# A trunk of two transformer layers on one core: adaLN weights ahead of x, a fourth query buffer, one held tile pair

## The chip, the core and the metric

The kernel runs on one core of one Trainium2 chip. Its time is the device time of one execution in microseconds (us). Three runs of the kernel before took 2890.32, 2893.75 and 2896.26 us; the median is 2893.75.

## The reference

Two layers of a diffusion trunk in float32: width 1024, 1024 latent tokens, 256 context tokens, feed-forward width 2816. Each layer takes six modulation vectors from a conditioning vector (adaLN), normalises, attends and runs a SwiGLU. Layer 0 attends in a sliding window, layer 1 in a neighbourhood of a 64-column grid; layer 1 leaves its context rows unchanged.

```python
h, hc = x, ctx
for i in range(2):
    sh1, sc1, gt1, sh2, sc2, gt2 = split(silu(c) @ w_ada[i] + b_ada[i], 6)
    # sh1c ... gt2c likewise from silu(c_ctx)
    a  = rms_norm(h, g_mix[i]) * (1 + sc1) + sh1
    ac = rms_norm(hc, g_mix[i]) * (1 + sc1c) + sh1c
    y, yc = (swa_mixer, na_mixer)[i](a, ac, ...)
    h = h + gt1 * y
    h = h + gt2 * swiglu(rms_norm(h, g_ffn[i]) * (1 + sc2) + sh2)
    # the context rows hc the same way, in layer 0 only
```

## The kernel before

Activations stand with the width on the 128 partitions and tokens in columns, in chunks of 512 tokens. Each float32 operand of a large product is split into a high and a low half (ACT writes the high one, the difference is taken by VectorE or POOL), and a product is three matmuls: high·high, high·low, low·high.

The stages follow each other in `run`: `front0` (modulation, projections), `attn0`, `back(0)` (output projection, feed-forward), `front1`, `attn1`, `back(1)`. All are written against pools of named tiles: `pool.tile(..., tag=, bufs=n)` gives one of n buffers, and whoever would fill a buffer waits until the last reader of its old content is done. A scheduler of the framework sets the order of instructions on each engine from the dependences, its own estimates and, where given, `high_priority`; `issue_after` keeps instructions behind another on their engine. The engines then run their own queues in order. SP (SyncE) issues nearly all transfers, one after the other.

Three places matter.

The start is `front0`. `load(0)` issues eight transfers of x (`xn`, 256 KB each) on SP; `stats` squares (ACT, L226 and L229) and adds (VectorE, L230); `modulate` sums over the partitions (PE, L238), takes the reciprocal root on POOL (L242), transposes (PE, L249) and then writes, for each of eight slices of 128 rows, a scaled tile `nt` (VectorE, L254), a high half (ACT, L259 or L263) and a low half `pr` (VectorE L260, or POOL L264). `ada_half(0, 0, half)` loads half of the first adaLN group, eight transfers of 512 KB (L176), and multiplies with the conditioning vector (L180), four products of 32 rows each for each of four steps, into one bank; `ada_close` copies it (ACT, L186), transposes (PE, L189) and adds the bias (VectorE, L196 to L202). `gsc` and `mod` from there are what `nt` and the halves are scaled and shifted with. `qkv_part` runs the first projections (PE, L354) on the halves. The rope tables are made on POOL (L425, L431).

In `attn1`, eight pairs of heads pass over eight query tiles of 128 tokens. `load_pair` loads values, the keys `kst1` of both heads (L667, three buffers) and the biases; `begin` loads the queries `qst1` of both heads for two query tiles at a time (L686 and L687, three buffers); `scores` multiplies (PE, L702 against the context's keys, L705 against the neighbourhood's) into a double bank `b2`, of which there are two, and takes the softmax (VectorE L710, ACT L712); `turn` transposes the probabilities (PE, L730); `finish` multiplies with the values (PE, L746) and the reciprocal sums (L752).

In `back`, gate and up are computed by a scheme that forms seven products of half-size blocks (`product`, PE L808) instead of eight. `first` makes the first two and keeps their results in two tiles `kp` (ACT, L967 and L970, eight buffers of the tag), `second` and `third` the other five. For the first NPRE = 6 of the 22 column blocks, `first` runs ahead of the others, since the second chunk of tokens is then still being normalised (L908). Of those six pairs, HELD stay in their tiles; the others are written to memory (L1026) and read back when their turn comes (L1040).

Of the kernel before, what the change touches and what calls it, by code (L numbers as in the profile page):

```python
# [12 lines left out]
F32R = mybir.dt.float32r  # L13
# [6 lines left out]
P = 128  # L20
# [30 lines left out]
def f32(ap):  # L51
    return ap.bitcast(F32)


class Trunk:
# [113 lines left out]
    def ada_half(self, layer, grp, half):  # L169
        nc = self.nc  # L170
        ps = self.bank()
        src = self.a["w_ada"][layer, :, grp * 2048:(grp + 1) * 2048].rearrange("(k p) (j n) -> k p j n", p=P, n=512)
        for k in range(4):
            w = [self.slot(F32) for _ in range(2)]
            for z in range(2):
                nc.sync.dma_start(out=w[z], in_=src[4 * z + k, :, half::2])  # L176
            for z in range(2):
                for i in range(2):
                    r = 64 * z + 32 * i
                    nc.tensor.matmul(ps[r:r + 32, :], self.cond[:, 4 * z + k, :], w[z][:, i], start=(k == 0), stop=(k == 3))  # L180
        self.ada_close(layer, grp, ps, [(half + 2 * i, (32 * i, 64 + 32 * i)) for i in range(2)])

    def ada_close(self, layer, grp, ps, parts):
# [184 lines left out]
    def front0(self):  # L368
        nc, tc, a = self.nc, self.tc, self.a
        with ExitStack() as cx:  # L370
# [3 lines left out]
            pool = self.pool(cx, "p1", 2)  # L374
# [3 lines left out]
            def load(c):  # L378
                c0, n = CH[c]
                for k in range(KT):  # L380
                    t = xpool.tile([P, 512], F32, name="x", tag="x")
                    nc.sync.dma_start(out=t[:, :n], in_=a["xn"][k * P:(k + 1) * P, c0:c0 + n])
                    xs[c, k] = t[:, :n]

            def stats(c):
                st = self.stat_start(tmp, CH[c][1], 2 - c // 2)
                for k in range(KT):
                    self.stat_add(st, xs[c, k])
                return st
# [3 lines left out]

            self.mod_pool = self.pool(cx, "p1m", MB)
            pts = [self.pair_tiles(c) for c in range(3)]
            load(0)
            sts = [stats(0)]
            mods = [modulate(0)]
            adv = lambda i, n: [next(mods[i]) for _ in range(n)]
            adv(0, 1)  # L400
            self.ada_half(0, 0, 0)
            adv(0, 4)
            units = [self.qkv_unit(0, 2, u) for u in range(2)]
            self.ada_half(0, 0, 1)
# [243 lines left out]
    def attn1(self):  # L648
        nc, tc, a = self.nc, self.tc, self.a
        with ExitStack() as cx:  # L650
            self.psum(cx, 4, 2)
            cx.enter_context(self.early)
            pool = self.early_pool
# [25 lines left out]
            def begin(pr, m):  # L679
                if m % 2 == 0:  # L680
                    qst = {}
                    for x in range(2):
                        h = 2 * pr + x
                        q = pool.tile([P, 2, 256], F32R, name="qst1", tag="qst1", bufs=3)
                        s = f32(self.qs[1][h * 64:(h + 1) * 64, :, m * P:(m + 2) * P])
                        nc.sync.dma_start(out=f32(q[0:64]), in_=s)  # L686
                        nc.sync.dma_start(out=f32(q[64:128]), in_=s)  # L687
                        qst[x] = q
                    cur["q"] = qst
                    cur["sm"] = self.small.tile([P, 2, 2], F32, name="sm1")  # L690
                    cur["two"] = {}
                lat = list(range(max(m - 1, 0), min(m + 2, 8)))
                return dict(cur, pr=pr, m=m, kts=lat + [8, 9] if m == 0 else [8, 9] + lat, nl=len(lat) * P, p=[], pt=[])
# [68 lines left out]
            for pr in range(8):  # L762
                load_pair(pr)
                for m in range(8):
                    if m % 2 == 1 and pr == 7:
                        self.wo_ahead.append(self.unit(a["w_o1"][len(self.wo_ahead)]))
                    u = begin(pr, m)
                    steps = list(range(0, len(prev["kts"]), 2)) if prev else []
                    for j in range(max(2, len(steps))):
                        if j < 2:  # L770
                            with tc.high_priority(offset=HP1):
                                scores(u, j)
                        if j < len(steps):
                            turn(prev, steps[j])
                    if old:
                        finish(old)
                    old, prev = prev, u
# [33 lines left out]
    def back(self, layer, o):  # L811
        nc, tc, a = self.nc, self.tc, self.a
# [165 lines left out]
        def weights(f):  # L978

            a11, a12, a21, a22 = load_gu(f, ((0, 0), (0, 1), (1, 0), (1, 1)))  # L980
            late = "vector" if f < NPRE else "gpsimd"
            if f >= NPRE:
                yield self.split(a11, xslot(), "vector"), self.split(a12, xslot(), "vector")
            s1 = self.add(wt(), a21, a22, ALU.add)
            s2 = sub(s1, a11)
            yield self.split(s2, xslot(), "vector")
            s3 = sub(a11, a21)
            rest = [self.split(x, xslot(), lo) for x, lo in ((s3, "vector"), (s1, late), (a22, late))]
            self.add(s2, a12, s2, ALU.subtract)
            yield rest + [self.split(s2, xslot(), late)]  # L990
# [15 lines left out]
            self.add(y1, y1, u3, ALU.mult)  # L1006
            nc.sync.dma_start(out=self.ss[layer][f, :, 512:1024], in_=y1)

        NPRE, HELD = 6, 2
        ew = []  # L1010
        for f in range(NPRE):
            a11, a12 = load_gu(f, ((0, 0), (0, 1)))
# [18 lines left out]
        for f in range(NF):  # L1031
            w = weights(f)
# [56 lines left out]
        for g in groups:  # L1089
            W = {f: self.unit(a["w_down"][layer, f * P:(f + 1) * P, :], alt(f), slot=self.slot if f > 1 else self.pslot) for f in g}  # L1090
            for c in range(2):
                acts = {}
                for f in g:
                    r = rawf()
                    nc.sync.dma_start(out=r, in_=self.ss[layer][f, :, c * 512:(c + 1) * 512])
                    w = self.split(r, self.pslot(), alt(f + 1))
# [185 lines left out]
```

## Time and profile before

| | |
|---|---|
| runs shown, median (us) | 2893.75 (2890.32 to 2896.26) |
| profiled execution, time (us) | 2896.47 |
| its span (us) | 2894.7 |
| its granted TensorE clock, mean | 0.992 |
| TensorE busy (us) | 2812.0 |
| VectorE, ACT, POOL busy (us) | 1645.7, 1119.7, 791.0 |
| HBM read, written (MB) | 317.73, 83.62 |

Times in the profile are microseconds from the start of the span. PE is TensorE, PEld its weight loads, DVE is VectorE, ACT ScalarE, POOL GpSimd, SP SyncE, and "SPq" work in SP's DMA queue. L354 is line 354 of the kernel before; three lines are added at L177, so that most lines of the kernel after have numbers higher by three. In a row of the timeline stand the start, the time until the last of the group ended, the engine, line and operation, the tile written and those read, shapes, and how many instructions the row holds; in brackets the idle time ahead of it and what ended that. In a row of waits stand the engine and line that waited, who ended it, the total in us, the times, and the longest.

### The profile page before, as it was taken

What the parts mean: (1) busy time and instruction counts of PE and PEld (TensorE: products, weight loads), DVE (VectorE), ACT (ScalarE), POOL (GpSimd) and SP (SyncE); (2) the same over time, 40 slices, a digit from 0 to 9 for tenths busy, and PEclk for the clock granted to TensorE, in tenths of its full rate; (3) what the DMA queues carried; (4) which work ended last, traced back from release to release, by engine and by line L of the source; (5) the groups of instructions that cost most, each with busy time, mean ns of one, the idle gap of its engine ahead of it and who ended that gap; (6) DMA issues with size and microseconds to landing.
All of it is one profiled execution on the core that took longest, in us unless ns stands there. A gap on an engine that the chain in (4) does not pass through costs nothing.

```text
span 2894.7 us, 42717 instructions
## 1 busy us (share of the span) xinstructions
PE 2812.0 (97%) x15586; PEld 2310.6 (80%) x15586; DVE 1645.7 (57%) x2965; ACT 1119.7 (39%) x2263; POOL 791.0 (27%) x802
## 2 busy tenths in 40 slices
PE   6999999999999999999999999999999999999999
PEld 3667777788888887778999888788788788887887
DVE  5657777658755555446543344166656856556442
ACT  4323666535223232234553222266654423233120
POOL 3443242210121222233873354111101021123220
PEclk8999999999999999999999999999999999999999
DMA  7583342434322248644563464366753422226221
GB/s 269 176 246 97 90 135 81 158 110 133 131 81 84 81 146 301 207 147 134 180 188 111 119 182 117 107 182 162 194 178 125 149 95 77 81 88 207 85 91 62
DMA packets 306178, 404.18 MB, mean 140 GB/s; under 512 B 30128, under 2 KB 165808, under 8 KB 305968
## 3 DMA queue, kind: packets, MB, share of 16 engines
q1 hardware_dynamic: 237072, 362.91, 39.7%
q10 hardware_dynamic: 68896, 38.55, 4.6%
q8 instruction: 123, 2.02, 0.3%
q14 instruction: 87, 0.71, 0.1%
HBM read 317.73 MB, written 83.62 MB: 139 GB/s over the span
## 4 chain that ended last, share of the span: by engine, by line
PE 87%; DMA 4%; DVE 4%; ACT 1%; issue 1%; POOL 1%; SPq 1%; DVEq 0%; ACTq 0%; POOLq 0%
PE b L808 17%; PE bm L1068 16%; PE bm L808 12%; PE bm L354 11%; PE bm L866 7%; PE bm L1129 4%; PE b L602 3%; PE b L354 3%; PE b L590 2%; PE b L1068 2%; DMA qst<-q_s 2%; PE b L730 2%; PE b L746 2%; PE b L557 1%; PE b L161 1%
## 5 line engine op out<-in xcount | busy, mean ns | idle before, releaser
L1068 PE MATMUL bm<-pr,wsp 128*128 128x512 f32 x1920 | 440.3, 390 | 0.0
L1068 PEld LDWEIGHTS bm<-pr,wsp 128*128 128x128 f32 x1920 | 359.2, 188 | 82.1 <-issue 5.9
L808 PE MATMUL b<-wsp,px 128*128 128x512 f32 x1584 | 377.9, 391 | 0.0
L808 PEld LDWEIGHTS b<-wsp,px 128*128 128x128 f32 x1584 | 297.5, 188 | 65.1
L848 DVE SCALAR_TENSOR_TENSOR px<-bm,mod,px 128x512 f32<-128x512 f32 (+1 forms) x232 | 170.7, 739 | 268.6 <-PE bm L1068 220.8
L808 PE MATMUL bm<-pr,px 128*128 128x512 f32 x1296 | 317.1, 392 | 5.2 <-ACT kp L970 5.2
L143 ACT CAST wsp<-raw 128x512 fp32r<-128x512 f32 x306 | 188.3, 620 | 342.5 <-PE bm L1068 116.3
L808 PEld LDWEIGHTS bm<-pr,px 128*128 128x128 f32 x1296 | 243.5, 188 | 59.3 <-ACT kp L970 6.1
L354 PE MATMUL bm<-wsp,pr 128*128 128x512 f32 x1152 | 272.4, 393 | 0.0
L144 POOL TENSOR_TENSOR px<-wt,px 128x512 fp32r<-128x512 f32 x64 | 91.1, 1424 | 628.5 <-ACT px L143 369.9
L354 PEld LDWEIGHTS bm<-wsp,pr 128*128 128x128 f32 x1152 | 213.4, 188 | 43.4
L144 POOL TENSOR_TENSOR wsp<-raw,wsp 128x512 fp32r<-128x512 f32 x132 | 174.7, 1331 | 250.4 <-ACT wsp L143 232.1
L143 ACT CAST px<-wt 128x512 fp32r<-128x512 f32 x176 | 108.3, 621 | 330.5 <-PE b L808 302.4
L144 DVE TENSOR_TENSOR wsp<-raw,wsp 128x512 fp32r<-128x512 f32 x174 | 141.2, 816 | 144.1 <-ACT wsp L143 143.0
L866 PE MATMUL bm<-pr,wsp 128*128 128x512 f32 x768 | 176.8, 390 | 0.0
L354 PE MATMUL b<-wsp,pr 128*128 128x512 f32 x576 | 148.8, 412 | 19.1 <-ACT pr L263 6.6
L866 PEld LDWEIGHTS bm<-pr,wsp 128*128 128x128 f32 x768 | 143.3, 188 | 29.3
L354 PEld LDWEIGHTS b<-wsp,pr 128*128 128x128 f32 x576 | 110.8, 198 | 56.2 <-issue 12.7
L710 DVE CUSTOM_DVE_ANT_0 pr<-b,wsp,big 128x640 f32<-128x640 f32 (+1 forms) x128 | 107.0, 847 | 83.9 <-PE b L705 71.5
L294 POOL TENSOR_TENSOR hrs<-hss,mhalf 128x8 f32<-128x8 f32 (+1 forms) x66 | 104.8, 1587 | 169.2 <-DVE hss L292 164.4
L1166 DVE TENSOR_TENSOR t<-b,kp 128x512 f32<-128x512 f32 x88 | 60.8, 691 | 135.5 <-PE b L808 135.2
L1129 PE MATMUL bm<-prc,wsp 128*128 128x256 f32 x1056 | 134.3, 285 | 0.0
(205 smaller groups left out, 4822.0 us busy)
## 6 DMA issues: line engine op xcount, KB each, us to landing
raw<-w_gu SPq DMA_DIRECT2D x156, 256.0 KB, 2.8
qst<-q_s SPq DMA_DIRECT2D x288, 128.0 KB, 3.1
rawf<-w_gu SPq DMA_DIRECT2D x132, 256.0 KB, 3.1
raw<-w_down SPq DMA_DIRECT2D x110, 256.0 KB, 3.3
wsp<-w_ada SPq DMA_DIRECT2D x48, 512.0 KB, 6.9
pr<-w_ada SPq DMA_DIRECT2D x48, 512.0 KB, 6.5
s_s<-t SPq DMA_DIRECT2D x88, 256.0 KB, 2.0
rawf<-s_s SPq DMA_DIRECT2D x88, 256.0 KB, 3.4
```

The costliest lines, as they stand in the source:

```text
L143: self.nc.scalar.copy(out=w[:, 0, :n], in_=x)
L144: getattr(self.nc, lo).tensor_tensor(out=w[:, 1, :n], in0=x, in1=f32(w[:, 0, :n]), op=ALU.subtract)
L294: nc.gpsimd.tensor_tensor(out=rs[:, :nh], in0=ss[:, :nh], in1=self.mhalf[:, :nh], op=ALU.pow)
L354: self.nc.tensor.matmul(ps, x, y, start=(k == 0 and i == 0), stop=(k == KT - 1 and i == 2))
L602: nc.tensor.matmul(op[64 * r:64 * r + 64, :256], u["v"][:, kts[i], :], u["pt"][i][:, 256 * r:256 * r + 256], start=(i == 0), stop=(i == n ...
L710: nc.vector.tensor_tensor_reduce(out=pt[:, :nl + 256], in0=V, in1=u["bias"][x][m // 7][:, b0:b0 + nl + 256], scale=-1.0, scalar=self.big, ...
L808: self.nc.tensor.matmul(ps, x, y, start=first and k == 0 and i == 0, stop=last and k == 3 and i == 2, skip_group_check=True)
L848: nc.vector.scalar_tensor_tensor(out=h[c, k], in0=ps, scalar=mod[:, ty, k, z:z + 1], in1=h[c, k], op0=ALU.mult, op1=ALU.add)
L866: nc.tensor.matmul(ps[:, :n], x, y, start=(k == 0 and i == 0), stop=(k == KT - 1 and i == 2))
L1068: nc.tensor.matmul(ps, x, y, start=(z == 0 and i == 0), stop=(z == len(parts) - 1 and i == 2))
L1129: nc.tensor.matmul(ps[:, q * CTX:(q + 1) * CTX], x, y, start=(k == 0 and i == 0), stop=(k == KT - 1 and i == 2))
L1166: self.nc.vector.tensor_tensor(out=out, in0=x, in1=y, op=op)
```

## The change

Four edits. In `ada_half`, the four products of a step are told to follow one another directly on PE, the second slot's pair first. In `front0`, `ada_half(0, 0, 0)` is written ahead of `load(0)`. In `attn1`, `qst1` has four buffers in place of three. In `back`, HELD is 1, so five pairs of the six are written and read back.

```diff
--- before.py
+++ after.py
@@ -174,10 +174,13 @@
             w = [self.slot(F32) for _ in range(2)]
             for z in range(2):
                 nc.sync.dma_start(out=w[z], in_=src[4 * z + k, :, half::2])
-            for z in range(2):
-                for i in range(2):
-                    r = 64 * z + 32 * i
-                    nc.tensor.matmul(ps[r:r + 32, :], self.cond[:, 4 * z + k, :], w[z][:, i], start=(k == 0), stop=(k == 3))
+            with ExitStack() as order:
+                for z in (1, 0):
+                    for i in range(2):
+                        r = 64 * z + 32 * i
+                        m = nc.tensor.matmul(ps[r:r + 32, :], self.cond[:, 4 * z + k, :], w[z][:, i], start=(k == 0), stop=(k == 3))
+                        if z and not i:
+                            order.enter_context(self.tc.issue_after(getattr(m, "ins", m)))
         self.ada_close(layer, grp, ps, [(half + 2 * i, (32 * i, 64 + 32 * i)) for i in range(2)])
 
     def ada_close(self, layer, grp, ps, parts):
@@ -393,12 +396,12 @@
 
             self.mod_pool = self.pool(cx, "p1m", MB)
             pts = [self.pair_tiles(c) for c in range(3)]
+            self.ada_half(0, 0, 0)
             load(0)
             sts = [stats(0)]
             mods = [modulate(0)]
             adv = lambda i, n: [next(mods[i]) for _ in range(n)]
             adv(0, 1)
-            self.ada_half(0, 0, 0)
             adv(0, 4)
             units = [self.qkv_unit(0, 2, u) for u in range(2)]
             self.ada_half(0, 0, 1)
@@ -681,7 +684,7 @@
                     qst = {}
                     for x in range(2):
                         h = 2 * pr + x
-                        q = pool.tile([P, 2, 256], F32R, name="qst1", tag="qst1", bufs=3)
+                        q = pool.tile([P, 2, 256], F32R, name="qst1", tag="qst1", bufs=4)
                         s = f32(self.qs[1][h * 64:(h + 1) * 64, :, m * P:(m + 2) * P])
                         nc.sync.dma_start(out=f32(q[0:64]), in_=s)
                         nc.sync.dma_start(out=f32(q[64:128]), in_=s)
@@ -1006,7 +1009,7 @@
             self.add(y1, y1, u3, ALU.mult)
             nc.sync.dma_start(out=self.ss[layer][f, :, 512:1024], in_=y1)
 
-        NPRE, HELD = 6, 2
+        NPRE, HELD = 6, 1
         ew = []
         for f in range(NPRE):
             a11, a12 = load_gu(f, ((0, 0), (0, 1)))
```

The order that the scheduler makes of it differs as follows at the places of which the prediction speaks. In SP's queue, at the start, `wsp` are the adaLN weights and `x` the tokens. Before:

```order
L85 DMA gm<-gains 128x32
L87 DMA bada<-b_ada 128x96
L382 DMA x<-xn 128x512 x8
L176 DMA wsp<-w_ada 128x2x512 x8
L131 DMA raw<-w_qkv 128x512 x3
L382 DMA x<-xn 128x512 x4
```

After:

```order
L85 DMA gm<-gains 128x32
L87 DMA bada<-b_ada 128x96
L176 DMA wsp<-w_ada 128x2x512 x8
L385 DMA x<-xn 128x512 x8
L131 DMA raw<-w_qkv 128x512 x3
L385 DMA x<-xn 128x512 x4
```

The two groups of eight have changed places. On POOL, at the start, `rot` and `rot_478` are the rope tables and `pr<-nt,pr` is a low half of the modulated tokens. Before:

```order
L242 TENSOR_TENSOR rs<-ss,mhalf 128x4
L144 TENSOR_TENSOR wsp<-raw,wsp 128x512
L425 TENSOR_TENSOR rot_478<-rot,gq 128x512
L264 TENSOR_TENSOR pr<-nt,pr 128x512
L431 TENSOR_TENSOR rot_478<-rot,gq 128x8x16 x4
L425 TENSOR_TENSOR rot<-rot,gq 128x512
L144 TENSOR_TENSOR wsp<-raw,wsp 128x512
L431 TENSOR_TENSOR rot<-rot,gq 128x8x16 x2
L264 TENSOR_TENSOR pr<-nt,pr 128x512
```

After:

```order
L144 TENSOR_TENSOR wsp<-raw,wsp 128x512
L245 TENSOR_TENSOR rs<-ss,mhalf 128x4
L428 TENSOR_TENSOR rot_478<-rot,gq 128x512
L434 TENSOR_TENSOR rot_478<-rot,gq 128x8x16 x4
L428 TENSOR_TENSOR rot<-rot,gq 128x512
L434 TENSOR_TENSOR rot<-rot,gq 128x8x16
L144 TENSOR_TENSOR wsp<-raw,wsp 128x512
L434 TENSOR_TENSOR rot<-rot,gq 128x8x16 x3
L267 TENSOR_TENSOR pr<-nt,pr 128x512 x2
```

A weight split stands ahead of the reciprocal root, and both tables stand ahead of the first low half. On PE, in `attn1`, at the first query tile of the second pair of heads, `kst_18083` and `kst_18092` (after: `kst_18089` and `kst_18098`) are the keys of the new pair's two heads, and the L730 rows transpose probabilities of the pair before. Before:

```order
L702 MATMUL b_18108<-kst_18083,qst_18101 128x256 x2
L705 MATMUL b_18108<-kst_18083,qst_18101 128x256 x2
L730 MATMUL b_18117<-ident,pr_18029 128x128
L730 MATMUL b_18117<-ident,pr_18045 128x128
L730 MATMUL b_18117<-ident,pr_18029 128x128
L730 MATMUL b_18117<-ident,pr_18045 128x128
L730 MATMUL b_18133<-ident,pr_18029 128x128
L730 MATMUL b_18133<-ident,pr_18045 128x128
L730 MATMUL b_18133<-ident,pr_18029 128x128
L730 MATMUL b_18133<-ident,pr_18045 128x128
L702 MATMUL b_18124<-kst_18092,qst_18104 128x256 x2
```

After:

```order
L705 MATMUL b_18114<-kst_18089,qst_18107 128x256 x2
L708 MATMUL b_18114<-kst_18089,qst_18107 128x256 x2
L705 MATMUL b_18130<-kst_18098,qst_18110 128x256 x2
L708 MATMUL b_18130<-kst_18098,qst_18110 128x256 x2
L733 MATMUL b_18123<-ident,pr_18035 128x128
L733 MATMUL b_18123<-ident,pr_18051 128x128
```

The second head's scores stand directly behind the first's, ahead of the eight transposes.

## Prediction

> **What bounds the kernel now.** I read the page's busy line and its chain first, then TensorE's waits over the whole span, then the timeline of the three places that the diff touches.
>
> ```profile
> PE 2812.0 (97%) x15586; PEld 2310.6 (80%) x15586; DVE 1645.7 (57%) x2965; ACT 1119.7 (39%) x2263; POOL 791.0 (27%) x802
> ...
> PE 87%; DMA 4%; DVE 4%; ACT 1%; issue 1%; POOL 1%; SPq 1%; DVEq 0%; ACTq 0%; POOLq 0%
> ...
> PE b L238 <- DVE acc L230: 15.2, 2, 13.0
> PE b L702 <- DMA qst<-q_s: 11.7, 12, 2.1
> PE b L354 <- ACT pr L263: 6.6, 2, 5.3
> ...
> PE bm L808 <- ACT kp L970: 5.2, 2, 2.6
> ...
> PE b L702 <- DVE ot L755: 1.2, 1, 1.2
> ```
>
> TensorE (PE) is busy for 97% of 2894.7 us, and the change leaves its instructions as they are; only idle time, or a low clock, can be won. All of it is 2894.7 − 2812.0 = 82.7 us, and the wait rows (line: us in total, times, longest) name what the diff reaches: 11.7 us in attention 2 for query tiles, 5.2 us in two pieces in the seven-product stage, and the start, where the wait on DVE `acc` and those around L354 lie.
>
> **Attention 2, the fourth query buffer.** The whole stage and its DMA queue:
>
> ```profile
> 1870.00:2128.00 258.00, 242.01 (x2415) 210.35 (x2415) 176.13 (x419) 172.17 (x419) 40.22 (x91) 1.00 0.61 164
> ...
> SPq L686 <- PE b L705: 85.8, 18, 38.8
> ...
> DMA to landing us min/median/max: 3.9/5.1/6.6
> ...
> DMA to landing us min/median/max: 3.9/4.4/4.8
> ```
>
> The columns of the first row are the window, its length, then busy time of PE, weight load, DVE, ACT and POOL, the granted clock (1.00) and the DMA share. PE idles 258.0 − 242.0 = 16.0 us, so no buffer here can bring more. The queue stands 85.8 us in front of query loads until scores (L705) free the third buffer: that is the cause of the 11.7 us. A fourth buffer lets both heads' next queries start one group of two query tiles earlier; such a group is 258/32 = 8.1 us, more than any landing in this stage took, so I take all 12 waits of 11.7 us as gone.
>
> What is late next? The keys `kst1`, which keep three buffers: at each of the seven boundaries between head pairs, the second head's keys are asked for only after the last use of a buffer of the pair before. The last two rows of the fence are the time from issue to landing of the key loads, in the whole stage and at the first boundary, which runs thus:
>
> ```profile
> 1898.23 1.11 SPq L667 DMA_DIRECT2D kst<-k_s  x2
> ...
> 1900.03 0.60 SPq L687 DMA_DIRECT2D qst<-q_s  x1
> ...
> 1902.74 0.48 PE L702 MATMUL b<-kst,qst 128*128 128x256 f32 x2
> 1903.30 1.04 PE L730 MATMUL b<-ident,pr 128*128 128x128 f32 x8
> ...
> 1905.99 0.48 PE L702 MATMUL b<-kst,qst 128*128 128x256 f32 x2 [1.65 <-DMA qst<-q_s]
> ```
>
> In the old order eight transposes (1.04 us) stand between the scores of the new pair's first head (1902.74) and those of its second; in the new order the second head's scores follow the first's at once, so PE asks for the second head's keys at 1903.30, not at 1904.34. Those keys are asked for at 1898.7 (second of the two issues) and land up to 4.8 us later, at 1903.5 to 1903.6: a wait of about 0.3 us remains. The same subtraction at the other six boundaries, each with its own landing, leaves 0.05, 0.3, 1.1, 0.4, 0.5 and 1.1 us; together 3.7 us. If all seven keys land as fast as the fastest (3.9), nothing is left; if all as late as the slowest (6.6), 1898.7 + 6.6 − 1903.3 = 2.0 us each, 14 us in all. I take 3.7, since it is the sum of landings that did occur, and the net is 11.7 − 3.7 = **8.0 us gained** (bounds: 11.7 + 1.2 for a wait put down to another engine, and −2.3).
>
> **The first adaLN weights ahead of x.** The rows of the start:
>
> ```profile
> 2.11 3.75 SPq L382 DMA_DIRECT2D x<-xn  x8
> 5.91 6.00 SPq L176 DMA_DIRECT2D wsp<-w_ada  x8
> ...
> 12.99 1.87 PE L238 MATMUL b<-ones,acc 128*128 128x2 f32 x8 [12.99 <-DVE acc L230]
> ...
> 15.21 1.02 POOL L242 TENSOR_TENSOR rs<-ss,mhalf 128x4 f32<-128x4 f32 x1 [13.91 <-DVE ss L240]
> ...
> 22.12 0.14 PEld L180 LDWEIGHTS b<-wsp,cond 128*32 128x32 f32 x4 [0.59 <-DMA wsp<-w_ada]
> ...
> 27.12 1.41 DVE L254 SCALAR_TENSOR_TENSOR nt<-x,gsc,b 128x512 f32<-128x512 f32 x2
> ...
> 29.85 2.07 PE L354 MATMUL b<-wsp,pr 128*128 128x512 f32 x4 [5.33 <-ACT pr L263]
> ...
> 31.04 1.71 POOL L264 TENSOR_TENSOR pr<-nt,pr 128x512 fp32r<-128x512 f32 x1
> ...
> 32.80 5.16 PE L354 MATMUL b<-wsp,pr 128*128 128x512 f32 x12 [0.88 <-POOL pr L264]
> ...
> 40.84 5.08 PE L354 MATMUL b<-wsp,pr 128*128 128x512 f32 x21 [1.04 <-POOL pr L264]
> ...
> 53.75 0.66 PE L189 MATMUL b<-ident,sb 128*128 128x128 f32 x4 [0.73 <-ACT sb L186]
> ```
>
> The swap moves 2 MB of x (8 × 256 KB) behind 4 MB of weights (8 × 512 KB) on SP's queue; `nt` (27.12) needs both, and both end near 22.1, where PE took up the last weights, either way. What follows the last landing differs. Before, it was the adaLN product, its copy, transposes and modulation sums: 22.1 to 27.1. After, it is the last Square and sum, the statistics product (L238, 1.9), the 1.0 us reciprocal root on POOL, now behind a 1.4 us weight split, and the transposes, which I put at the root's 1.0; I walk this to `nt` at about 28.5, and with the same hi half behind it to a first projection product near 32.0 in place of 29.85. On POOL, the rope tables move ahead of the first lo half:
>
> ```profile
> 29.42 1.66 POOL L425 TENSOR_TENSOR rot<-rot,gq 128x512 f32<-128x512 f32 x1 [2.56 <-DVE gq L420]
> ...
> 32.71 2.16 POOL L431 TENSOR_TENSOR rot<-rot,gq 128x128 f32<-128x128 f32 x4
> 34.84 1.27 POOL L425 TENSOR_TENSOR rot<-rot,gq 128x512 f32<-128x512 f32 x1
> 36.07 1.75 POOL L144 TENSOR_TENSOR wsp<-raw,wsp 128x512 fp32r<-128x512 f32 x1
> 37.79 1.77 POOL L431 TENSOR_TENSOR rot<-rot,gq 128x128 f32<-128x128 f32 x2
> ```
>
> Before, the first lo half stood behind one of these (ready at 32.75); after, behind 1.66 + 2.16 + 1.27 + 1.75 and four L431 at 0.89 (3.5), 10.4 us, and its own 1.3. From about 28.0, when VectorE has scaled `gq`, that is 39.7, seven microseconds later, and near the 40.84 at which PE took up its second lo half before. Products held back by it: 44 at 5.08/21 = 0.24 us, 10.6 us, with three groups of four adaLN products at about 1.0: 39.7 + 10.6 + 3.0 = 53.3. PE comes from a pause, and the clock comes in:
>
> ```profile
> 32.00:36.00 4.00, 3.20 (x8) 2.52 (x9) 2.62 (x4) 1.92 (x4) 4.00 (x6) 0.50 0.96 301
> 36.00:38.00 2.00, 2.00 (x10) 1.34 (x12) 2.00 (x2) 1.09 (x2) 2.00 (x3) 0.64 1.06 407
> 38.00:40.00 2.00, 1.80 (x12) 0.28 (x10) 1.61 (x3) 1.01 (x2) 2.00 (x3) 1.00 1.04 392
> ```
>
> The last column but two is the granted clock: 0.50 until PE has run without a break from 32.80 to about 37.4, 4.6 us that do 2.3 us of work: 53.3 + 2.3 = 55.6 against 53.75, **1.8 us lost** at the transposes (L189) on which the second half of the modulation hangs. [...]
>
> Keeping the column tiles together pays some of it back: four kept together take 1.0 us, and before, the second half ran its 16 in six pieces, now in four; that is already in the three groups above. The copy that the transposes waited for (0.73) has other products behind which to stand. I give back 0.8 us: **1.0 us lost** at the start. Bounds: 2 us gained, if the first lo half comes at 36.7, with POOL's tables begun 3 us sooner; 4 us lost, if the clock stays at half for over twice the 4.6 us.
>
> **One held pair in the seven-product stage.** Four more transfers of 256 KB go out per layer and come back (two each way), on SP's queue. The wait that holding two pairs could be the cause of:
>
> ```profile
> 682.14 0.72 ACT L908 ACTIVATE px<-px,mod 128x512 f32<-128x512 f32 x1 [1.08 <-DVE px L900]
> ...
> 688.96 0.57 ACT L970 ACTIVATE kp<-bm 128x512 f32<-128x512 f32 x1
> 689.59 0.79 PE L808 MATMUL bm<-pr,px 128*128 128x512 f32 x1 [2.61 <-ACT kp L970]
> ...
> 689.50:692.70 3.20, 3.11 (x7) 2.44 (x8) 3.20 (x7) 3.20 (x8) 0.00 (x0) 0.50 0.43 164
> ...
> kp<-u_s SPq DMA_DIRECT2D x16, 256.0 KB, 3.5
> ```
>
> PE's bank waits for an evacuation (L970) that stands in ACT's in-order queue behind modulation work; ACT runs without a gap from 682.14 to 688.96. No kept tile is awaited there, and in both programs PE, ACT and DVE have the same order up to it. So the 2.61 us, and the half clock behind it (3.2 us at 0.50, 1.6 us of work), stay in both layers. Behind this wait PE has no gap in the stage, so the reload of the second pair costs **nothing** while it lands before its use, and the pair before it has seven products to cover it. If that cover is gone, the price is one landing, the last row's 3.5 us, in one layer or in both. Bounds: 0.5 gained, 7 lost; I take 0, because PE waits for no reload of the pairs that are spilled already.
>
> **The sum.** −8.0 + 1.0 + 0 = −7.0. The profiled execution took 2896.47 (span 2894.7 and 1.8 around it), 2.7 above the median of the runs, 2893.75; I take the difference from the median: **2886.8 us**.
>
> **Rivals.**
> - *Everything gained.* The keys are hidden, because early queries leave the queue to them: 11.7 + 1.2 and a start that costs 1: 2893.75 − 11.9 = 2881.9. For: in the old order each key load stood behind query loads at its boundary. Against: landings of up to 6.6 us under a DMA share of 0.61.
> - *The keys take it back.* At each boundary 1.5 us for keys, 10.5 in all; with the start at 1 the result is 2893.5, no change. For: the new order asks earlier. Against: only one of the seven subtractions comes to over 1.1.
> - *Slower.* The new order puts both heads' scores side by side, where transposes stood between them, and there are two double banks: the next scores wait until a softmax pass (L710) has read one. If each of the 64 units of a pair and a query tile pays 0.22 us, the loss of 14.1 is over the 8.0 gained by 6.1, and with the start at 1 it is 2900.8. It decides from (8.0 − 1.0 + 5.8)/64 = 0.20 us a unit. Against: VectorE is busy 176.1 of 258 us, and the longest of PE's waits on it there is the 1.2 us above.
> - *The held pair was the wait.* If its two kept tiles hold ACT up, 5.2 us and twice 1.6 of clock go too: 8.4 more, 2878.4. Against: ACT had no gap.
> - *The start gains.* The adaLN work off the last landing is worth more than the lo half costs: 3 us gained in place of 1 lost, 2882.8. Against: the lo row.
>
> **Chances.** Forecast, net gain between 4 and 11: 0.52. Everything gained 0.12, keys take it back 0.15, slower 0.08, held pair 0.06, start gains 0.07. About 0.2%, 5.8 us, is what a measurement of this kernel can tell from no change; so faster begins at 2888.0. My forecast lies only 1.2 us beyond it: of its 0.52, 0.34 is faster and 0.18 same. Faster: 0.34 + 0.12 + 0.06 + 0.07 and 0.02 of the keys' case, 0.61; same: 0.18 + 0.12, 0.30, slower: 0.08 and 0.01 of the keys' case, 0.09. The range leaves out slower, held pair and a quarter of the keys' case: 2879.5 to 2893.0.
>
> **What would show it.** In the profile after: the wait of L705 (was L702) on `qst` gone or below 1 us, a new one on `kst` of 3 to 4 us at boundaries; PE busy in the attention window unchanged at 242 with 8 us less span; the wait on ACT `kp` still 5.2 in two pieces; the transposes of the first column's second half at 55 to 56. Wrong if `kst` waits exceed 8 us, if DVE appears as a releaser of scores, or if the start moves by over 4 us.

## The result, and the profile after

The changed kernel took 2874.29 us, the median of four runs (2872.16 to 2878.33), against 2895.01 for the kernel before beside it: a ratio of 0.9934 (95% interval 0.9922 to 0.9946), 20.7 us faster. Forecast were 7 us and a range of 2879.5 to 2893.0. A second set of five runs (e9 below) gave 0.9930 (0.9917 to 0.9942). The page's busy line and its chain, after:

```profile
PE 2805.8 (98%) x15586; PEld 2307.1 (80%) x15586; DVE 1641.8 (57%) x2965; ACT 1117.6 (39%) x2263; POOL 789.0 (27%) x802
...
PE 87%; DVE 3%; DMA 2%; ACT 1%; issue 1%; POOL 1%; SPq 0%; DVEq 0%; ACTq 0%; POOLq 0%
```

TensorE does the same work in a span of 2871.4 instead of 2894.7 us: 65.6 us of idle time where there were 82.7, and 6 us less at work. On the chain, transfers fall from 4% to 2% and VectorE from 4% to 3%. Four of PE's waits over the span (line: us in total, times, longest); the first is the start, where PE now waits for weights before it waits for x:

```profile
PE b L181 <- DMA wsp<-w_ada: 12.8, 5, 8.3
...
PE bm L811 <- ACT kp L973: 5.2, 2, 2.6
...
PE b L749 <- ACT ptt L516: 4.0, 1, 4.0
...
PE b L705 <- DMA kst<-k_s: 0.7, 1, 0.7
```

No wait for query tiles is left at L705 (11.7 us before, at L702). The wait in the seven-product stage is the same 5.2 us, the row on keys reads 0.7 us and not 3.7, and the wait of 4.0 us at L749 was 0.5 us before (L746). The window of attention 2, with the columns of the row shown for before:

```profile
1857.00:2107.00 250.00, 242.58 (x2425) 213.09 (x2424) 174.87 (x420) 171.11 (x421) 40.41 (x91) 0.99 0.65 169
```

To see where the 20 us came from, the span is cut at instructions that both programs have: the transposes of the second adaLN half (L189), the first scores of attention 1 (L557), its last product (L602), the first scores (L702) and the last product (L746) of attention 2. Lengths in us, worked out from PE's first and last instruction of each stage, for before, after and the kernels with some of the four edits:

| kernel | to L189 | rest of the first stage | attention 1 | attention 2 |
|---|---|---|---|---|
| before | 53.8 | 216.0 | 278.9 | 254.2 |
| e4, one held | 53.9 | 217.6 | 273.3 | 254.5 |
| e3 and e13, four query buffers | 53.9, 54.2 | 215.3, 214.8 | 276.8, 276.1 | 242.4, 241.0 |
| e2, tiles together | 52.9 | 216.0 | 273.9 | 257.6 |
| e1, weights first | 55.8 | 211.2 | 274.2 | 254.8 |
| e15, both at the start | 53.2 | 209.1 | 274.1 | 255.8 |
| e5, after with three query buffers | 54.7 | 209.4 | 275.4 | 253.0 |
| after and e9 | 53.2, 53.2 | 209.8, 209.5 | 273.7, 275.6 | 244.4, 244.3 |

The stages that are left out differ by at most 4 us between any two of these kernels, and follow no edit. Attention 2 is 253 to 258 us with three query buffers and 241 to 244 with four. The rest of the first stage is 215 to 218 with x loaded first and 209 to 211 with the weights first. Attention 1 differs by 5.6 us between before and e4, whose orders are the same on every engine up to there: that part of the difference between the two first profiles (5.2 us) belongs to no edit.

### The profile page after: what moved, and what is told of

It is laid out like the page before. It is cut to its first block, busy times and chain, and to the rows that moved or that the text cites. A ratio compares the mean times of both kernels' runs of the same rounds, so it can differ in the third digit from the quotient of the medians.

```text
span 2871.4 us, 42752 instructions
## 1 busy us (share of the span) xinstructions
PE 2805.8 (98%) x15586; PEld 2307.1 (80%) x15586; DVE 1641.8 (57%) x2965; ACT 1117.6 (39%) x2263; POOL 789.0 (27%) x802
## 4 chain that ended last, share of the span: by engine, by line
PE 87%; DVE 3%; DMA 2%; ACT 1%; issue 1%; POOL 1%; SPq 0%; DVEq 0%; ACTq 0%; POOLq 0%
PE b L811 16%; PE bm L1071 16%; PE bm L811 12%; PE bm L357 11%; PE bm L869 7%; PE bm L1132 4%; PE b L605 3%; PE b L749 3%; PE b L733 2%; PE b L593 2%; PE b L1071 2%; PE b L357 2%; PE b L708 1%; PE b L560 1%; PE b L705 1%; PE b L562 1%
## 5 line engine op out<-in xcount | busy, mean ns | idle before, releaser
L357 PE MATMUL b<-wsp,pr 128*128 128x512 f32 x576 | 147.3, 410 | 12.5 <-ACT kv L440 5.3
```

The source lines that it names most:

```text
L357: self.nc.tensor.matmul(ps, x, y, start=(k == 0 and i == 0), stop=(k == KT - 1 and i == 2))
```

## The experiments

**The four edits one at a time.** e1: the call of `ada_half(0, 0, 0)` ahead of `load(0)`.

```diff
+            self.ada_half(0, 0, 0)
             load(0)
...
-            self.ada_half(0, 0, 0)
```

> Only ada_half(0, 0, 0) is written ahead of load(0). Theory A (what the changed kernel gained ahead of attention 2, 12 to 13 us of span, comes from the new order at the start): 8 to 12 us faster than before, the waits at 111.6 (weights, 2.27 us) and at 151.0 (1.89 us) gone, first scores of attention 1 at 263 to 265 instead of 269.8. Rival B (these stalls come and go from run to run, whatever the kernel): no difference in the median, and the half-clock intervals behind the stalls fall in other places. Rival C (the order at the start gains only through the column tiles): within 2 us of before.

Measured: 2889.53 us against 2893.58, ratio 0.9981 (0.9972 to 0.9990). The start is 2 us longer, the stage behind it 5 us shorter. Theory A's waits are gone, its size is about half; rival B falls for this stage: every kernel with x first and the stage otherwise unchanged shows these waits, and in those with the weights first the wait for the weights and the later of the two on `hx` are gone, and the other is 0.6 us or less (0.9 in e16 and 1.1 in e12). PE's waits between 54 and 270 us, of before:

```profile
PE b L354 <- DVE hx L298: 4.4, 6, 1.9
PE b L161 <- DMA wsp<-w_ada: 2.5, 2, 2.3
```

The same view of e1, in which L161 is not named any more:

```profile
PE b L354 <- DVE hx L298: 1.8, 5, 0.6
```

e2: the column tiles alone.

```diff
-            for z in range(2):
-                for i in range(2):
+            with ExitStack() as order:
+                for z in (1, 0):
+                    for i in range(2):
...
+                        if z and not i:
+                            order.enter_context(self.tc.issue_after(getattr(m, "ins", m)))
```

> Only the column tiles of the adaLN half product are kept together; x is still loaded ahead of the weights. Theory A: 0 to 3 us faster, since only the second half's sixteen products change their place (six pieces become fewer), and the start up to 37 us with its 10.2 us at half clock stays. Rival C: 8 to 12 us faster, with the waits at 111.6 and 151.0 gone. Rival B: no difference in the median.

Measured: 2892.64 us, ratio 0.9993 (0.9985 to 1.0002), 1 us at L189 and nothing behind it (the wait at 111 us is 2.57, that at 150 us 1.63), which is what theory A expected and rival C did not. What the 1 us is, two rows of the timeline of before show: two products (x4, since the trace counts two matmuls for each, 64 at L180 for 32 products) take as long as four (x8).

```profile
45.85 1.05 PE L180 MATMUL b<-wsp,cond 128*32 128x512 f32 x4
...
51.95 1.06 PE L180 MATMUL b<-wsp,cond 128*32 128x512 f32 x8
```

e3: four query buffers alone; e13 is the same kernel again.

```diff
-  q = pool.tile([P, 2, 256], F32R, name="qst1", tag="qst1", bufs=3)
+  q = pool.tile([P, 2, 256], F32R, name="qst1", tag="qst1", bufs=4)
```

> Only qst1 has four buffers. Theory A: attention 2 is 8 to 10 us shorter, its query waits (12, 11.7 us) gone, and everything ahead of it is as before: the half-clock intervals near 27, 112, 372 and 392 us are there again. Rival B: one or more of these intervals is missing, though the order ahead of attention 2 is unchanged. A wait of about 4 us on an ACT copy near the last pair of heads, as in the changed kernel, if it comes from the early queries; if it is missing, it came from somewhere else.

> Only four query buffers, again. Theory A (the whole gain lies in attention 2, 10 to 12 us): 2880 to 2883 us. Rival N (it is larger than the stage shows, as the first six runs had it): 2876 to 2879 us. Attention 2 at 242 to 245 us in both.

Measured: 2878.27 against 2893.58 us, ratio 0.9945 (0.9930 to 0.9960); again 2880.05 against 2895.93, 0.9949 (0.9936 to 0.9963). This edit is three quarters of the whole. PE's waits of e3 in attention 2:

```profile
PE b L746 <- ACT ptt L513: 2.3, 1, 2.3
PE b L702 <- DMA kst<-k_s: 1.5, 3, 0.9
PE b L702 <- DVE mn L710: 1.1, 2, 0.9
```

The query waits are gone, the key waits are small. The two ratios mean 15 to 16 us, and the stage itself is 11.8 and 13.2 us shorter than before's; the interval of the second, 10.7 to 18.5 us, holds both.

e4: one held pair.

```diff
-        NPRE, HELD = 6, 2
+        NPRE, HELD = 6, 1
```

> Only HELD is 1. As predicted: within 1 us of before, the waits on ACT kp at L808 2.6 us in each layer as before. The rival (the held pair caused these waits): 5 to 9 us faster. Rival B: half-clock intervals ahead of the seven-product stage differ from before, though its order is unchanged.

Measured: 2893.71 us, ratio 1.0001 (0.9991 to 1.0010), and the wait on ACT `kp` unchanged at 5.2 us in two pieces. Nothing, as forecast.

**Do they add up?** e5 is the changed kernel with `bufs=3` again, e15 the kernel before with both edits at the start.

> The changed kernel with three query buffers again. Theory A (the edits add up: four query buffers 12 to 15 us, the two edits at the start 4 to 6, the held pair 0): 4 to 6 us faster than before, attention 2 at 254 to 257 us as before. Rival D (the start's edits gain only together, and the query buffers less than they did alone): 8 to 12 us faster than before.

> The two edits at the start alone (weights first, column tiles together), three query buffers, two held pairs. If edits add up: 5 to 7 us faster than before, the stage between 54 and 270 us at 209 to 211 us instead of 215 to 218, attention 2 as before.

Measured: e5 2887.11 against 2893.32 us, 0.9978 (0.9969 to 0.9988); e15 2886.70 against 2895.93, 0.9966 (0.9956 to 0.9976): 6 and 10 us, with intervals that overlap; e15 is above its expected 5 to 7. With the query buffers' 15 that makes 21 to 25, against 20.7 measured, so a plain sum is good enough. Rival D is not borne out, as e1 gained without the tiles and e5's median lies below 8 us; that a few microseconds come only from the two edits together is not excluded, since e5's interval reaches 9 us and e15's 13.

**Early loads, or another order of scores?** With four buffers the scheduler also orders the scores otherwise, so e10 and e14 keep the buffers and make the second head's load wait, e10 for a POOL copy of the previous group's reciprocal sums (`rx`), e14 for its plain sums.

```diff
+   if x and "last" in cur:    # e10; cur["last"] is the previous rx
+       nc.gpsimd.tensor_copy(out=q[0:1, 0, 0:1], in_=cur["last"][0:1, 0:1])
+   if x and "sm" in cur:      # e14, in place of these two lines
+       nc.gpsimd.tensor_copy(out=q[0:1, 0, 0:1], in_=cur["sm"][0:1, 1, 0:1])
    nc.sync.dma_start(out=f32(q[0:64]), in_=s)
```

> The changed kernel with its four query buffers, but the second head's query load waits for a POOL copy of the previous group's reciprocal sums, which is about as late as three buffers let it start. Theory I (the gain is the earlier start of the query loads): the query waits return, attention 2 is 252 to 258 us, 8 to 13 us slower than the changed kernel. Rival J (the gain comes from the scheduler's other order of scores, which four buffers bring): within 3 us of the changed kernel.

> The changed kernel with four query buffers, the second head's query load held back until the previous group's sums of the first head are there, earlier than in e10 by one softmax and a reciprocal. Theory I (the start of the query loads is what counts): the loss is much smaller than e10's 79 us, 5 to 25 us, and the stage has waits on qst again. Rival J (the scheduler's order of scores): within 3 us of the changed kernel, or as slow as e10.

Measured: e10 2951.59 us, 1.0204 of before (1.0190 to 1.0218); e14 2912.75 us, 1.0065 (1.0052 to 1.0077): 79 and 39 us slower than the changed kernel, both far more than expected; attention 2 takes 318.3 and 279.1 us. PE's waits of e14 in attention 2, now at L707:

```profile
PE b L707 <- issue: 15.3, 9, 4.3
PE b L707 <- DMA qst<-q_s: 10.3, 7, 2.3
PE b L735 <- ACT pr L717: 4.1, 14, 0.3
```

The query waits are back (10.3 us here, 10.6 in e10), near the 11.7 us of before, and the longer hold costs more; rival J's "within 3 us" falls. But the hold also made the scheduler order the scores anew, and most of the loss is in waits that neither kernel has. So it is shown that query loads held back bring the query waits back; how much of the gain the new order has by itself is not shown, and no kernel here has the one without the other.

**The wait of 4 us on a copy.** It stands in the timeline of after, in the last pair of heads. With three query buffers it is 0.8 us or less; with four buffers alone it is 2.3 us (e3) and 2.0 (e13), so it comes with the fourth buffer:

```profile
2052.43 2.04 SPq L131 DMA_DIRECT2D raw<-w_o  x3
...
2059.40 0.62 ACT L143 CAST wsp<-raw 128x512 fp32r<-128x512 f32 x1 [4.76 <-DMA raw<-w_o]
...
2060.23 0.36 ACT L516 COPY ptt<-b 128x256 f32<-128x256 f32 x1
...
2060.64 2.00 PE L749 MATMUL b<-ptt,v 128*64 128x128 f32 x20 [4.00 <-ACT ptt L516]
```

PE waits for a copy; the copy stands behind a cast of the next stage's weight in ACT's queue and began 0.2 us after that cast ended, and ahead of the cast ACT has idled for 4.76 us until the cast's transfer landed, 6.9 us after its issue, behind keys, biases and queries. e6 takes these weights ahead from query tile 3 of the last pair on, e7 and e11 write the first of them one pair earlier.

```diff
-   if m % 2 == 1 and pr == 7:
+   if m % 2 == 1 and pr == 7 and m > 1:                                    # e6
+   if (m % 2 == 1 and pr == 7 and m > 1) or (pr == 6 and m == 7):          # e7, e11
```

> The changed kernel, but in the last pair of heads the first output weights are taken ahead from query tile 3 on, not from tile 1 (three units ahead instead of four). Theory E (the 4 us wait on ACT's copy near 2060 us is a weight cast standing in ACT's in-order queue until its transfer has landed behind biases, keys and the now earlier queries): that wait and the half clock behind it go, attention 2 is 3 to 6 us shorter than 244.4, and 2 to 5 us of it stay in the whole. Rival F (ACT is simply short of time there): the wait stays, or moves, and the time is within 2 us of the changed kernel.

> The changed kernel, but the first unit of output weights is written in the pair before the last, so four units stay ahead. Theory E: the order of transfers puts this weight behind the biases all the same, so the cast waits as before if it stands at the same place in ACT's queue: 0 to 3 us faster. Rival F: no change.

> The changed kernel once more, beside the next three on the same chip. 2872 to 2878 us, attention 2 at 244 to 245 us with the wait on ACT's copy of about 4 us near 2060.

> The changed kernel with the first unit of output weights written one pair of heads earlier, beside the changed kernel. Theory E (its cast no longer stands in ACT's queue ahead of a copy that PE needs): attention 2 at 240 to 242 us, no half clock there, 3 to 6 us faster than the changed kernel. Rival K (its one shorter profile was chance): the same as the changed kernel within 2 us.

Measured: e6 2876.51 us, and its wait stays (3.04 us): the first cast still stood ahead of the copy that PE needs, and its transfer landed at 2062.0, so the edit moved nothing that counts. e7 2873.44 and e11 2873.76 us; the wait is gone in both, and attention 2 is 240.6 and 240.9 us. PE's waits of e11 there:

```profile
PE b L705 <- DVE mn L713: 1.9, 3, 0.9
PE b L705 <- DMA kst<-k_s: 1.3, 3, 0.9
```

That the cast in ACT's queue is the cause is shown by these two against e6: the wait goes only where the cast no longer stands there. Yet the whole gains nothing that these runs tell: e9, the changed kernel beside e11, took 2872.54 us (2869.91 to 2875.53), e11 2870.34 to 2876.14. Their ratios to before, 0.9930 and 0.9935, each have an interval of about 4 us to either side, so a gain as small as the stage's 3.6 us is neither shown nor excluded.

**The wait on ACT `kp`.** e12 takes e11 and moves eight additions of `norm_lat` from ACT to POOL, e16 four of them.

```diff
-   nc.scalar.activation(out=h[1, k], in_=h[1, k], func=AF.Identity, bias=sh[:, k, 0:1])
+   nc.gpsimd.tensor_scalar(out=h[1, k], in0=h[1, k], scalar1=sh[:, k, 0:1], scalar2=None, op0=ALU.add)
```

> As the one before, and the eight additions of a shift to the second chunk's tokens in back (ACT, L908's neighbour) are done by POOL, which is idle there. Theory L (the wait of 2.6 us on ACT kp in each layer is ACT's in-order queue of modulation work, whatever is held): both waits shrink to under 1 us, with their half clock, 4 to 9 us faster than the kernel before it. Rival M (POOL's slower additions come late for combine): a new wait on DVE or POOL in the products behind, and no gain or a loss.

> As e12, but only four of the eight shift additions go to POOL. Theory L: the waits on ACT kp shrink to about 1 us and no new wait of 1.9 us on DVE takes their place; 2 to 6 us faster than the changed kernel. Rival M: the wait is shared out between ACT and DVE as in e12, no gain.

Measured: e12 2871.89 us, 0.9929 (0.9916 to 0.9941) of before; e16 2872.05 us, 0.9918 (0.9904 to 0.9931). PE's waits of e12 in that stage of layer 0:

```profile
PE bm L811 <- DVE pr L144: 1.9, 1, 1.9
PE bm L811 <- ACT kp L973: 0.7, 1, 0.7
PE bm L811 <- DVE px L144: 0.5, 1, 0.5
```

ACT's wait falls from 2.6 to 0.7 us when its queue is shorter, which is theory L's mechanism, and VectorE's splits are late next: 3.1 us in all, rival M's result. e16 shares 1.4 and 1.6. Both ratios lie within the interval of the changed kernel's second set (0.9917 to 0.9942); none is shown to beat it.

**Is the stall at 111 us the gain at the start?** e8 leaves the start as before and begins the background adaLN products two query tiles later.

```diff
-                if layer == 0 and (ci or t > 2):
+                if layer == 0 and (ci or t > 4):
```

> The kernel before, with the start untouched, but the background adaLN products of the first stage begin two query tiles later. Theory G (of the 4.9 to 6.3 us that the weights-first order gained between 54 and 270 us, most is the weight wait near 111 us of 2.3 to 2.6 us, the two waits on DVE hx near 142 and 151, and their half clock): these waits shrink or go with the start as before, and the stage is 2 to 6 us shorter. Rival H (the gain comes from the start's new order itself): the stage keeps its 215 to 218 us.

Measured: 2890.33 us, 0.9990 (0.9981 to 0.9998). The waits on `hx` fell from 4.4 to 1.0 us, the weight wait stayed (2.5), and the stage kept 215.5 us, as rival H has it; but PE worked 2.2 us longer in it, where the products came in more and smaller pieces (two took as long as four in the rows under e2, 1.05 and 1.06 us), and the longest of the waits that G is about did not go. So e8 does not tell G from H. That the stage gains through these waits is read from the traces (from before to after its idle time falls from 18.4 to 12.5 us, its length from 216.0 to 209.8, and the two wait rows shown for before lose 5.2 us together); no experiment took them away alone, so this cause is argued and not shown.

## Why the prediction was wrong, point by point

**The query buffers: right mechanism, mis-sized.** The term was −8.0, from −11.7 for query waits and +3.7 for keys. The query waits went in full, but 11.7 us was too small a price for them. The idle time in a row begins at the end that the profile gives the instruction ahead, and that end can lie behind the start of the next one, here by 0.24 us. Two rows of after, with nothing awaited:

```profile
2073.50 1.03 PE L733 MATMUL b<-ident,pr 128*128 128x128 f32 x8
2074.29 0.48 PE L705 MATMUL b<-kst,qst 128*128 128x256 f32 x2
```

The scores start 0.79 us behind the first of eight transposes, though the row of the eight lasts 1.03. By that step the scores of 1905.99 in before were 1.90 us late, where the row says 1.65. Counted from start to start in the same way, the twelve query waits of before cost some 14.5 us (an estimate from the steps of ten profiles). Two waits on VectorE (`ot` 1.2 and `ri` 0.9 us) went too.

The key term held better than its row tells. At all seven boundaries of after, the second head's keys landed 4.6 to 5.3 us after their issue, and its scores started 0.1 to 0.25 us behind the landing: the keys did become the next thing that was late. Start to start this makes some 2.9 us in after, and 2.5 to 3.5 in e3, e13 and e9, close to the 3.7 of the walk; the rows (0.7 to 2.2 us) leave out the part ahead of the end that the profile gives and waits under 0.15 us, and put two of the waits of after down to other causes.

The copy behind the cast (2.0 to 4.0 us, with half clock behind it in after, 0.50 from 2061.2 to 2064.5, in e9, 0.68 from 2063.5 to 2067.0, and in e3, 0.99 over the stage where before has 1.00) is a wait that the prediction did not have, and it goes the other way. Together the stage is 10 to 13 us shorter than before's, where 8.0 was forecast, and the runs with four buffers alone give 15 to 16. The last 3 us lie within what two profiles can differ by, and are not located.

**The start: right to its end, and ended too early.** At L189 the term was +1.0 (1.8 for the order, −0.8 for the tiles); measured are +2.0 for the weights alone (e1), −0.9 for the tiles alone (e2), and −0.6 to +1.6 in the profiles with both (e15 and e6 the extremes). The first low half came at 37.6 and not at 39.7 (the first of the two in the POOL row):

```profile
32.38 2.08 PE L357 MATMUL b<-wsp,pr 128*128 128x512 f32 x4 [3.23 <-ACT pr L266]
...
36.37 2.49 POOL L267 TENSOR_TENSOR pr<-nt,pr 128x512 fp32r<-128x512 f32 x2
...
38.60 3.86 PE L357 MATMUL b<-wsp,pr 128*128 128x512 f32 x12
```

The step of the prediction that failed is that the walk of the start stopped at L189 and put what lies behind at nothing. The order of PE's instructions differs up to some 140 us; there the adaLN weights' wait (2.3 to 2.6 us) and two waits on `hx` (1.1 to 1.3 and 1.6 to 1.9 us) stand in the profiles with x first; with the weights first the first and the last are gone, and mostly 0.6 us or less is left of the other. In the stage that is 5 to 7 us by the table, for which the sum had no term; in the runs, the edits at the start gained 6 us (e5) and 10 us (e15) where 1 us lost was forecast. "The start gains" was a rival at 0.07, but argued from the last landing and not from what lies behind.

**The held pair: right.** Term 0, measured 1.0001 (0.9991 to 1.0010); the wait is ACT's queue, as e12 shows by shortening it.

**The range.** Its lower end, 2879.5, left out that two terms could err to the same side. Of the signs to look for, the vanished `qst` wait, PE's unchanged work in the window of attention 2 and the unchanged `kp` wait came. The row on keys was smaller than forecast, and the transposes came at 53.2, 1.8 us ahead of the 55 to 56 that were forecast.

## What to carry to other kernels

A walk of a reordered start must go on to the last instruction whose order differs, not to the first point at which both kernels meet. Here the buffer that lets loads start earlier removed all waits on them (11.7 us), and the next-late tile could be bounded from its own landing times; a wait of TensorE is better priced from start to start than by its row (an estimated 14.5 us against 11.7). What the buffer brought in exchange was a late load of the next stage: a cast that waited for it in ACT's queue held up a copy that has nothing to do with it, for 4.0 us of PE's time. And waits of TensorE of 2.0 to 2.5 us were mostly dearer than their length, by the half clock that followed 26 of 29 of them.

## What the runs showed of the hardware

**Half clock followed 26 of 29 waits of 2.0 to 2.5 us.** In ten profiles (before, after, e1 to e8), PE's waits that began at full clock between 60 and 2870 us were followed within 5 us of PE's stop by a stretch of granted clock 0.50 (each stretch counted for the last wait ahead of it) in 1 of 116 cases at 0.5 to 1.0 us, 1 of 60 at 1.0 to 1.5, 14 of 35 at 1.5 to 2.0, 26 of 29 at 2.0 to 2.5, 19 of 27 at 2.5 to 3.0, and 4 of 6 above. Ten of the 14 are one place, a wait of 1.97 us at the first scores of attention 1 that stands close behind another of some 1.5 us, so the length of one wait is not all that counts. A stretch lasted 3.41 us, sometimes 6.83, so where PE worked through it, it cost an estimated 1.7 or 3.4 us, half of its length at 0.50; it began mostly 2 to 3.5 us after PE stopped (13 of the 16 counted of before and after). One wait of 1.9 us, for queries in e2, and the window behind it:

```profile
1899.03 0.47 PE L705 MATMUL b<-kst,qst 128*128 128x256 f32 x2 [1.88 <-DMA qst<-q_s]
...
1900.40:1903.70 3.30, 3.30 (x26) 2.53 (x23) 0.99 (x4) 0.81 (x2) 0.00 (x0) 0.50 0.04 11
```

**Much of the spread between runs goes with the granted clock.** The same wait of 2.2 us at the end of layer 0 was followed by 6.83 us at half clock in the profile of before and by 3.41 in that of after:

```profile
1368.70:1375.40 6.70, 6.70 (x31) 6.70 (x32) 3.13 (x5) 3.02 (x7) 5.92 (x5) 0.50 0.48 161
```

```profile
1357.40:1364.10 6.70, 6.70 (x45) 6.70 (x45) 2.87 (x5) 3.49 (x7) 6.20 (x5) 0.75 0.47 154
```

Over the 71 runs of the kernel before that were taken beside the experiments (2886.4 to 2899.9 us) the mean time goes with the mean granted clock: 2898.1 us at 0.990 (6 runs), 2896.6 at 0.991 (16), 2893.2 at 0.992 (31), 2891.9 at 0.993 (14), 2888.6 at 0.994 (4). From 0.990 to 0.994 that is 9.5 us, and 0.004 of 2893 us is 11.6. One profile against one profile is good to some 5 us in this kernel, an estimate from this spread and from the 5.6 us in attention 1.

**At the start of after, the row of the granted clock does not fit the durations.** Four products of one shape took 2.07 us at 29.85 in before, where the row reads 0.50, and 2.08 us at 32.38 in after (above), where it reads 1.00:

```profile
32.30:34.50 2.20, 2.08 (x4) 1.17 (x4) 2.17 (x3) 1.10 (x3) 2.20 (x3) 1.00 1.01 344
```

Both are 0.52 us for one, where the 21 products of the same shape at 40.84 in before took 0.24 us each. The first clock record of after stands at 40.4 us; what the clock was ahead of it is read here from the durations, not from the row.
